# Token sums of the up-projection made ahead and kept in DRAM, in a hybrid block of 2,048 frames

## The chip, the cores and the metric

The kernel runs on one core of one Trainium2 chip. Its time is device microseconds for one launch, the median of several runs. Engines go by their names in the profile: PE (matrix products), DVE, ACT and POOL (elementwise work), SP (here the issuer of DMAs).

## The reference, cut to what matters

```
h  = h + concatenate([hgrn2(...), s5(...)]) @ w_out        # out tiles
hn = rmsnorm(h, ffn_norm_g)                                # (2048, 1024)
hid = hn @ w_up                                            # (1024 -> 2 x 2816)
hid = conv_b + sum(pad[:, j:j + seq_len] * conv_w[j] for j in range(3))
gate, val = split(hid, 2)
h  = h + (silu(gate) * val) @ w_down
```

All of it is float32.

## The kernel before, in words

The mixers run up to about 690 us, and then the projection with `w_out`. It goes in four blocks of 512 tokens, each of four out tiles (`out_tile`, 128 tokens, 48 matmuls). An out tile adds the residual, sums squares for the root mean square, and writes the tile to `h_d`. At the end of a block twelve operations on 128x4 (`rsqrt_mean`) make the scales `rst` of its tokens.

The up-projection runs in two halves of 1,024 tokens, 22 units each (`unit(hf, f)`). A unit makes 128 columns of the gate and 128 of the value. It does so with seven products, P1 to P7, of sums of weights and sums of tokens, in place of eight (Strassen's scheme in Winograd's form). With the tokens of a half in four parts B11, B12, B21 and B22 (first index: half of the model dimension; second: block of 512 tokens), the token factors are B11, B21, B22 and T1 = B12 − B11, T2 = B22 − T1, T3 = B22 − B12, T4 = B21 − T2. All factors stay in SBUF for a whole half, each as four tiles of 128x512 (index q). A matmul takes a float32 as a rounded part `h` and a rest `l`: `split` makes `h` by a copy on ACT and `l` by a subtraction on DVE or POOL. A product is twelve matmuls (four parts of the contraction by hh, lh and hl), so a unit has 84. `ps_u`, `ps_v` and `ps_w` are the PSUM banks of a unit: P1, P6, P7 and P4 go to u, P5 and P3 to v, P2 to w. P4 may start only when DVE has added P7 out of u (L62, `cv<-cv,ps_u`). `FACTOR` says which token factor a product takes: P1 B11, P2 B21, P5 T1, P6 T2, P3 B22, P7 T3, P4 T4.

The tokens come from `h_d`. For the first half, `h_load(0)` loads four tiles of 128x1024 during block 3's out tiles, ACT scales them, and `block_flips` turns them with PE (eight groups of four transposes, two in each out tile) and splits them as B11 and B21 (`nh`, `nl`). The other block of the half is turned in unit 0 by `token_sums`, four groups in P1 and four in P2, and for each q the sums are made: five on DVE and one on POOL, the splits of T1, T2 and T4 on DVE and those of B22 and T3 on POOL. For the second half the same is done in unit 21 (`block_flips`) and in the first unit of that half (`token_sums`). I call this place the change of tokens.

The sums of weights of the next unit are made during a unit by `unit_weights`: four sums (`us`) on POOL, five of the seven splits on DVE and two on POOL. The first unit's are made behind the last out tile (`first_up`).

A recording layer takes all operations, and a scheduler sets the order in which each engine gets them; from there every engine works in order. SP issues its DMAs in order too. `x_tile` has four buffers.

What PE needs of one q goes through load, scale, transposes, eviction, sum and split, in this order. The sum and split of T1 are:

```
sub(t1, b12, h11)
sub(t1, t1, l11)
part("T1", q, t1, VE)
```

## Time and profile before

| | us |
|---|---|
| median of 3 runs | 2310.33 (2306.52 to 2311.77) |
| the profiled execution | 2313.69 |
| its span in the trace | 2311.9 |
| PE busy | 2207.9 |
| DVE busy | 1712.9 |
| ACT busy | 990.7 |
| POOL busy | 765.6 |

The mean granted clock of PE is 0.977 of full speed. Where PE is busy without a break, the span is as long as its matmuls. Where it is not, the waits say which semaphore came last.

Stretches are told by the first matmul of a unit: block 3's out tiles begin at 845.95 us, unit 0 at 898.28, unit 4 at 1007.97, unit 21 at 1336.19, unit 26 (the fifth of the second half) at 1471.22, unit 43 at 1799.43.

### The profile page before, as it was taken

What the parts mean: (1) busy time and instruction counts of PE and PEld (TensorE: products, weight loads), DVE (VectorE), ACT (ScalarE), POOL (GpSimd) and SP (SyncE); (2) the same over time, 40 slices, a digit from 0 to 9 for tenths busy, and PEclk for the clock granted to TensorE, in tenths of its full rate; (3) what the DMA queues carried; (4) which work ended last, traced back from release to release, by engine and by line L of the source; (5) the groups of instructions that cost most, each with busy time, mean ns of one, the idle gap of its engine ahead of it and who ended that gap; (6) DMA issues with size and microseconds to landing.
All of it is one profiled execution on the core that took longest, in us unless ns stands there. A gap on an engine that the chain in (4) does not pass through costs nothing.

```text
span 2311.9 us, 28187 instructions
## 1 busy us (share of the span) xinstructions
PE 2207.9 (96%) x10120; PEld 1771.8 (77%) x10120; DVE 1712.9 (74%) x2615; ACT 990.7 (43%) x1770; POOL 765.6 (33%) x696
## 2 busy tenths in 40 slices
PE   8999999999989998899999988999999899999996
PEld 6778778888868876688888866888888677777775
DVE  9887786666664325887777778777777688788787
ACT  5333353232254334555555564555555423233343
POOL 1111100000000004555555555655555234445432
PEclk9899999999999999899999988999999999999998
DMA  6465655334434333222222222222222622222223
GB/s 226 143 210 178 188 183 162 124 125 131 141 87 136 116 119 109 83 97 83 83 80 82 78 91 82 93 82 82 83 82 73 227 83 84 71 90 75 68 88 119
DMA packets 143790, 262.18 MB, mean 113 GB/s; under 512 B 43936, under 2 KB 67360, under 8 KB 143648
## 3 DMA queue, kind: packets, MB, share of 16 engines
q1 hardware_dynamic: 138896, 243.05, 32.4%
q0 software_dynamic: 4752, 17.30, 2.0%
q8 instruction: 80, 1.31, 0.2%
q14 instruction: 62, 0.51, 0.1%
HBM read 178.52 MB, written 81.79 MB: 113 GB/s over the span
## 4 chain that ended last, share of the span: by engine, by line
PE 72%; DVE 16%; issue 5%; DMA 3%; ACT 2%; POOL 1%; SPq 0%; DVEq 0%; POOLq 0%; ACTq 0%
PE ps_u L1168 19%; PE ps_v L1168 9%; PE ps_out L975 6%; PE ps_du L1361 6%; PE ps_pj L231 5%; PE ps_pj L233 5%; PE ps_pj L232 5%; PE ps_w L1168 5%; PE ps_dv L1361 3%; DVE accp L62 2%; DVE gvl L65 2%; PE ps_dn L1448 1%; DMA graw<-gv_d 1%; DVE cv L65 1%; PE ps_att L649 1%
## 5 line engine op out<-in xcount | busy, mean ns | idle before, releaser
L231 PE MATMUL ps_pj<-xh,wh 128*128 128x512 f32 x640 | 261.9, 409 | 6.6 <-ACT xh L201 6.4
L232 PE MATMUL ps_pj<-xl,wh 128*128 128x512 f32 x640 | 256.4, 401 | 0.0
L233 PE MATMUL ps_pj<-xh,wl 128*128 128x512 f32 x640 | 256.0, 400 | 0.0
L74 DVE SCALAR_TENSOR_TENSOR cv<-cv,par 128x1024 f32<-128x1024 f32 x176 | 237.1, 1364 | 25.3 <-ACT cv L1180 23.4
L132 ACT ACTIVATE uh<-us 128x512 fp32r<-128x512 f32 x176 | 110.5, 630 | 195.6 <-PE ps_u L1168 93.4
L56 POOL TENSOR_TENSOR us<-uraw 128x512 f32<-128x512 f32 x88 | 121.8, 1384 | 215.4 <-DMA uraw<-in_wup_dram 149.7
L65 DVE TENSOR_TENSOR ul<-us,uh 128x512 fp32r<-128x512 f32 x132 | 156.2, 1184 | 1.6 <-ACT uh L132 1.5
L1361 PE MATMUL ps_du<-dh,gvh 128*128 128x512 f32 x320 | 131.9, 412 | 25.3 <-DVE accp L62 16.8
L132 ACT ACTIVATE uh<-uraw 128x512 fp32r<-128x512 f32 x132 | 83.5, 632 | 159.0 <-PE ps_u L1168 81.0
L231 PEld LDWEIGHTS ps_pj<-xh,wh 128*128 128x128 f32 x640 | 121.9, 190 | 37.2 <-ACT xh L201 6.4
L233 PEld LDWEIGHTS ps_pj<-xh,wl 128*128 128x128 f32 x640 | 121.6, 190 | 29.5 <-issue 1.1
L232 PEld LDWEIGHTS ps_pj<-xl,wh 128*128 128x128 f32 x640 | 121.7, 190 | 28.2 <-issue 1.5
L1361 PE MATMUL ps_du<-dl,gvh 128*128 128x512 f32 x320 | 128.6, 402 | 0.0
L1361 PE MATMUL ps_du<-dh,gvl 128*128 128x512 f32 x320 | 128.6, 402 | 0.0
L65 POOL TENSOR_TENSOR ul<-us,uh 128x512 fp32r<-128x512 f32 x44 | 68.6, 1560 | 173.0 <-ACT uh L132 170.6
L132 ACT ACTIVATE gvh<-gs 128x512 fp32r<-128x512 f32 x80 | 50.4, 630 | 162.3 <-POOL gs L56 81.6
L62 DVE TENSOR_TENSOR accp<-accp,ps_du 128x1024 f32<-128x1024 f32 (+1 forms) x84 | 97.7, 1163 | 28.7 <-PE ps_du L1361 28.3
L1180 ACT ACTIVATE cv<-cv,par 128x1024 f32<-128x1024 f32 x88 | 109.7, 1246 | 19.3 <-DVE cv L62 17.9
L56 POOL TENSOR_TENSOR gs<-graw 128x512 f32<-128x512 f32 x38 | 58.6, 1542 | 160.8 <-DMA graw<-gv_d 135.0
L1361 PEld LDWEIGHTS ps_du<-dh,gvh 128*128 128x128 f32 x320 | 61.7, 193 | 48.9 <-issue 23.8
L975 PE MATMUL ps_out<-wo,ogp 128*128 128x512 f32 x384 | 95.5, 404 | 0.9 <-DVE og L74 0.9
L515 POOL MEMSET z<- 128x4 f32 x16 | 1.7, 104 | 284.7 <-DVE zi L65 212.7
(438 smaller groups left out, 6237.4 us busy)
## 6 DMA issues: line engine op xcount, KB each, us to landing
uraw<-in_wup_dram SPq DMA_DIRECT2D x86, 512.0 KB, 3.5
gv_d<-cv SPq DMA_DIRECT2D x43, 512.0 KB, 2.6
graw<-gv_d SPq DMA_DIRECT2D x84, 256.0 KB, 3.3
wraw<-in_win_dram SPq DMA_DIRECT2D x24, 512.0 KB, 4.5
xt<-in_wdown_dram SPq DMA_DIRECT2D x44, 256.0 KB, 3.0
ws_d<-wh POOLq DMA_DIRECT2D x16, 512.0 KB, 3.5
ws_d<-wl POOLq DMA_DIRECT2D x16, 512.0 KB, 6.0
wh<-ws_d SPq DMA_DIRECT2D x16, 512.0 KB, 4.0
```

Source lines behind the costliest of these rows:

```text
L56: eng.tensor_tensor(o, a, b, op=op)
L62: eng.tensor_tensor(o, a, b, op=ALU.add)
L65: eng.tensor_tensor(o, a, b, op=ALU.subtract)
L74: eng.scalar_tensor_tensor(o, a, s, b, op0=op0, op1=op1)
L132: SC.activation(h, raw, AF.Copy)
L231: PE.matmul(ps, a, xh, start=(kt == 0), stop=False)
L232: PE.matmul(ps, a, xl, start=False, stop=False)
L233: PE.matmul(ps, b, xh, start=False, stop=(kt == KT - 1))
L975: PE.matmul(pss[nh], parts[lp][kt][:, tq], wo[rp][kt][:, nh * BLK : (nh + 1) * BLK], start=first, stop=last)
L1168: PE.matmul(ps, l, r[kt], start=(fresh and first), stop=end, skip_group_check=not fresh)
L1180: SC.activation(c, cin[:, 2 : HALF + 2], AF.Identity, scale=tap[2], bias=par[:, C_CB + cb : C_CB + cb + 1])
L1361: PE.matmul(ps[:, i], l[:, j, i * P : (i + 1) * P], r, start=(fresh and n == 0), stop=(n == 5), skip_group_check=not fresh)
```

## The change

New functions make the token sums apart from the place where they are used.

- `token_rows(hf, q)` does one q for both blocks of a half: it loads columns q and q+4 of the model dimension (128 each) for eight tiles of tokens (eight DMAs of 128x2x128, 128 KB, with ACT's scale of 256 columns behind each), turns them (four groups of four transposes, each with one ACT eviction), makes T1, T2, T4 and T3 with four subtractions on DVE, and writes T1, T2, B22, T3, T4 to `tr_d` in DRAM. For the first half B11 and B21 are split at once; for the second they are written too.
- `token_load` reads a tensor back, two tiles of 128x1024 each; `token_split` splits it, on ACT and DVE, in four parts.
- First half: the four q are made in the four out tiles of block 3. T1 and T2 are loaded back ahead of unit 0, and B22, T3 and T4 in unit 0. The sums and the two POOL splits of the first unit's weights go to DVE. The mean square of block 3 is recorded behind unit 0.
- Second half: q = 0 to 3 are loaded in units 2, 6, 10 and 14 and turned and summed in units 3, 7, 11 and 15. In unit 21 and the first unit of the second half there are only loads and splits: 28 of 128x512, all on DVE, with as many copies on ACT.

The diff:

```diff
--- before.py
+++ after.py
@@ -81,6 +81,8 @@
     h_d = dp.tile([SEQ, D], F32, name="h_d")
     gv_d = dp.tile([NF, P, SEQ], F32, name="gv_d")
     ws_d = [dp.tile([P, 2, KT * P], F32, name=f"ws_d{i}") for i in range(16)]
+    tr_d = [{k: dp.tile([P, 4, BLK], F32, name=f"tr_{k}{hf}") for k in ("B11", "B21", "T1", "T2", "B22", "T3", "T4")}
+            for hf in range(2)]
     m_d = dp.tile([8, 32 * 8 * (MS - 16) + MS], F32, name="m_d")
     tb_d = dp.tile([8, 4, P, 512], F32, name="tb_d")
 
@@ -114,19 +116,6 @@
 
     def halves(t):
         return [t[:, 0:BLK], t[:, BLK:D]]
-
-    def block_flips(xs, gcol, dst, pool, tag):
-
-        def one(kt):
...
     def split(raw, h, l, eng=GP):
         SC.activation(h, raw, AF.Copy)
@@ -985,16 +974,54 @@
             SC.activation(junk, xt[:, q], AF.Square, accum_out=ss[:, nh, i : i + 1])
         dma(h_d[t0 : t0 + P, :], xt)
 
-    def h_load(blk):
-
-        hs = []
-        for i in range(4):
-            t = 4 * blk + i
-            ht = x_tile()
-            dma(ht, h_d[t * P : (t + 1) * P, :])
-            SC.activation(ht, ht, AF.Copy, scale=rst[:, t : t + 1])
-            hs.append(halves(ht))
-        return hs
+    def token_rows(hf, q, pool, tag, first=None):
+
+        x, b = [], []
+
+        def load():
+            for j in range(2):
+                xt = x_tile().rearrange("p (i k c) -> p i k c", i=4, k=2)
+                for i in range(4):
+                    t = 8 * hf + 4 * j + i
+                    dma(xt[:, i], h_d[t * P : (t + 1) * P, :].rearrange("p (k q c) -> p k q c", k=2, q=4)[:, :, q])
+                    SC.activation(xt[:, i], xt[:, i], AF.Copy, scale=rst[:, t : t + 1])
+                x.append(xt)
+
+        def turned(j):
+            b.append(halves(x_tile()))
+            for k in range(2):
+                ps = pool.tile([P, BLK], F32, tag=tag, name="ps_x")
+                for i in range(4):
+                    PE.transpose(ps[:, i * P : (i + 1) * P], x[j][:, i, k], ident)
+                g = par[:, C_FFG + q + 4 * k : C_FFG + q + 4 * k + 1]
+                SC.activation(b[j][k], ps, AF.Copy, scale=g)
+
+        def sums():
+            (b11, b21), (b12, b22) = b
+            t1, t2 = halves(x_tile())
+            t3, t4 = halves(x_tile())
+            sub(t1, b12, b11)
+            sub(t2, b22, t1)
+            sub(t4, b21, t2)
+            sub(t3, b22, b12)
+            for k, t in dict(T1=t1, T2=t2, B22=b22, T3=t3, T4=t4).items():
+                dma(tr_d[hf][k][:, q], t)
+            for k, t in enumerate((b11, b21)):
+                if first:
+                    split(t, first[0][k][q], first[1][k][q], VE)
+                else:
+                    dma(tr_d[hf][("B11", "B21")[k]][:, q], t)
+
+        return [load, lambda: turned(0), lambda: turned(1), sums]
+
+    def token_load(hf, k):
+
+        rows = []
+        for p in range(2):
+            xt = x_tile()
+            dma(xt.rearrange("p (q t) -> p q t", q=2), tr_d[hf][k][:, 2 * p : 2 * p + 2])
+            rows += halves(xt)
+        return rows
 
     p3w = ExitStack()
     W3 = {}
@@ -1002,7 +1029,7 @@
 
     MAKE = ("P1", "P5", "P6", "P2", "P7", "P3", "P4")
 
-    def unit_weights(g, v):
+    def unit_weights(g, v, eng_s=GP):
 
 
 
@@ -1019,14 +1046,14 @@
 
         def summed(k, a, b, op, eng):
             s = tmp[k] = pool.tile([P, BLK], F32, tag="st", name="us", bufs=3)
-            tt(GP, s, a, b, op)
+            tt(eng_s, s, a, b, op)
             put(k, s, eng)
 
         ops = {
             "P1": lambda: put("P1", g[0], VE),
-            "P5": lambda: summed("P5", v[0], v[1], ALU.add, GP),
+            "P5": lambda: summed("P5", v[0], v[1], ALU.add, eng_s),
             "P6": lambda: summed("P6", tmp["P5"], g[0], ALU.subtract, VE),
-            "P2": lambda: put("P2", g[1], GP),
+            "P2": lambda: put("P2", g[1], eng_s),
             "P7": lambda: summed("P7", g[0], v[0], ALU.subtract, VE),
             "P3": lambda: summed("P3", g[1], tmp["P6"], ALU.subtract, VE),
             "P4": lambda: put("P4", v[1], VE),
@@ -1047,7 +1074,7 @@
         p2w.close()
         W3["pool"] = p3w.enter_context(tc.tile_pool(name="fw", reuse_waits="tile", bufs=2))
         r = W3["raw"]
-        W3["w"], ops = unit_weights(r[0:2], r[2:4])
+        W3["w"], ops = unit_weights(r[0:2], r[2:4], VE)
         for op in ops:
             op()
 
@@ -1055,7 +1082,7 @@
     parts[0] = og_parts(0)
     for cb in range(4):
         glu_out(y0, cb, pglu[cb], parts[0])
-    hn = [None, None]
+    hn = None
     for b in range(4):
         ss = sm.tile([P, 2, 4], F32, tag="hss", name="hss")
         weave = ()
@@ -1067,9 +1094,16 @@
                 raw = mx.tile([P, BLK], F32, tag=f"z{j % 2}{j // 2}", name="uraw")
                 dma(raw, A["wup"][j // 2].rearrange("p k c -> p (k c)")[:, (j % 2) * BLK : (j % 2 + 1) * BLK])
                 W3["raw"].append(raw)
-            hs = h_load(0)
-            hn[0] = first_tiles()
-            weave = block_flips(hs, C_FFG, hn[0], ps_s5, "s5")
+            hn = first_tiles()
+            rows = [token_rows(0, q, ps_s5, "s5", hn) for q in range(4)]
+            rows[0][0]()
+            weave = []
+            for q in range(4):
+                weave += [rows[q][1], rows[q][2]]
+                if q < 3:
+                    weave.append(lambda q=q: (rows[q][3](), rows[q + 1][0]()))
+                else:
+                    weave.append(rows[q][3])
         for i in range(4):
             out_tile(b, i, parts[b], ss, weave[4 * i : 4 * i + 4], first_up if (b, i) == (3, 3) else None)
             if b < 3:
@@ -1078,14 +1112,15 @@
                     gp = y_split(y)
                 for cb in ((), (0,), (1,), (2, 3))[i]:
                     glu_out(y, cb, glu_mm(gp, cb, ps_pj, "pj"), parts[b + 1])
-            elif i == 1:
-                hs = h_load(1)
         if b < 3:
             o = og_parts(b + 1)
             for p in range(2):
                 parts[b + 1][p] = o[p] + parts[b + 1][p]
         add(ss[:, 0], ss[:, 0], ss[:, 1])
-        rsqrt_mean(ss[:, 0], 4, D, "h", out=rst[:, 4 * b : 4 * b + 4])
+        rms = lambda b=b, ss=ss: rsqrt_mean(ss[:, 0], 4, D, "h", out=rst[:, 4 * b : 4 * b + 4])
+        if b < 3:
+            rms()
+    ahead = {k: token_load(0, k) for k in ("T1", "T2")}
     p2.close()
 
     if dbg == 2:
@@ -1107,53 +1142,13 @@
         def wide():
             return fx.tile([P, HALF + 2], F32, tag="cv", name="cv")
 
...
-        def token_sums(xs, first, tok):
-
-            tok.update({k: [[t[:, q] for q in range(4)] for t in
-                            (fb.tile([P, 4, BLK], F32R, tag=f"{k}{p}", name=f"t{k}{p}") for p in "hl")]
-                        for k in ("T1", "T2", "T3", "T4", "B22")})
...
+        def token_split(rows, k, dst):
+
+            if k not in dst:
+                t = [fb.tile([P, 4, BLK], F32R, tag=f"{k}{p}", name=f"t{k}{p}") for p in "hl"]
+                dst[k] = [[t[p][:, q] for q in range(4)] for p in range(2)]
+            for q in range(4):
+                split(rows[q], dst[k][0][q], dst[k][1][q], VE)
 
         FACTOR = {"P1": "B11", "P2": "B21", "P3": "B22", "P4": "T4", "P5": "T1", "P6": "T2", "P7": "T3"}
         NORMAL = ("P1", "P5", "P6", "P2", "P7", "P3", "P4")
@@ -1217,9 +1212,27 @@
             tok["B11"] = [first[p][0] for p in range(2)]
             tok["B21"] = [first[p][1] for p in range(2)]
 
+        def coming(hf, dst, order):
+
+            got = {}
+
+            def one(n):
+                if n:
+                    token_split(got.pop(order[n - 1]), order[n - 1], dst)
+                if n < len(order):
+                    got[order[n]] = token_load(hf, order[n])
+
+            return [(lambda n=n: one(n)) for n in range(len(order) + 1)]
+
+        for k in ("T1", "T2", "B22", "T3", "T4"):
+            for p in "hl":
+                fb.tile([P, 4, BLK], F32R, tag=f"{k}{p}", name=f"t{k}{p}")
         tok = {}
-        first_block(tok, hn[0])
-        sums = token_sums(hs, hn[0], tok)
+        first_block(tok, hn)
+        for k in ("T1", "T2"):
+            token_split(ahead[k], k, tok)
+        rest = coming(0, tok, ("B22", "T3", "T4"))
+        rows = [token_rows(1, q, ps_c, "x") for q in range(4)]
         w = W3["w"]
         for hf in range(2):
             for f in range(NF):
@@ -1230,20 +1243,26 @@
                 else:
                     w_next, ops = None, []
                 weave = {}
-                if f == 0:
-                    weave = {"P1": sums[0:4], "P2": sums[4:8]}
+                if f == 0 and hf == 0:
+                    weave = {k: [op] for k, op in zip(("P1", "P2", "P5", "P6"), rest)}
+                elif f == 0:
+                    weave = {"P1": [rest[5]], "P2": [rest[6]], "P5": [rest[7]]}
                 elif last and hf == 0:
-                    hs = h_load(2)
-                    nxt = first_tiles()
-                    fl = block_flips(hs, C_FFG, nxt, ps_c, "x")
-                    weave = {"P5": fl[0:2], "P6": fl[2:4], "P3": fl[4:6], "P7": fl[6:8]}
+                    nxt = {}
+                    first_block(nxt, first_tiles())
+                    rest = coming(1, nxt, ("B11", "B21", "T1", "T2", "B22", "T3", "T4"))
+                    rest[0]()
+                    weave = {k: [op] for k, op in zip(("P5", "P6", "P7", "P4"), rest[1:5])}
+                elif hf == 0 and f % 4 == 2 and f < 18:
+                    weave = {"P4": [rows[f // 4][0]]}
+                elif hf == 0 and f % 4 == 3 and f < 19:
+                    weave = {"P1": [rows[f // 4][1]], "P5": [rows[f // 4][2]], "P6": [rows[f // 4][3]]}
                 unit(hf, f, w, tok, EDGE if f == 0 or last else NORMAL, ops, weave)
                 w = w_next
+                if (hf, f) == (0, 0):
+                    rms()
                 if last and hf == 0:
-                    hs = h_load(3)
-                    tok = {}
-                    first_block(tok, nxt)
-                    sums = token_sums(hs, nxt, tok)
+                    tok = nxt
         pa.close()
```

Three places of the engines' order follow. The tiles `ul` are rests of weights, `us` the sums of weights, `tT1l` and the like rests of token factors, `cv` sums or convolution results, `x_...` a tile of the residual.

DVE behind the last out tile, before:

```order
L62 TENSOR_TENSOR x_8003<-x_8003,ps_out 128x512 x2
L65 TENSOR_TENSOR ul<-uraw,uh 128x512
L65 TENSOR_TENSOR ul<-us,uh 128x512 x3
L65 TENSOR_TENSOR ul<-uraw,uh 128x512
L62 TENSOR_TENSOR hss<-hss 128x4
L71 TENSOR_SCALAR rs_v<-hss 128x4
L69 TENSOR_SCALAR rs_i<-rs_v 128x4
L65 TENSOR_TENSOR ul<-uraw,uh 128x512
L71 TENSOR_SCALAR rst<-rs_i 128x4
L65 TENSOR_TENSOR cv<-cv,nh 128x512
L74 SCALAR_TENSOR_TENSOR rs_t<-rst 128x4
```

DVE ahead of and in unit 0, now:

```order
L65 TENSOR_TENSOR ul<-uraw,uh 128x512
L59 TENSOR_TENSOR rs_t<-rs_t,rs_v 128x4
L74 SCALAR_TENSOR_TENSOR rst<-rs_t,rst 128x4
L65 TENSOR_TENSOR tT1l<-xt,tT1h 128x512 x4
L65 TENSOR_TENSOR tT2l<-xt,tT2h 128x512 x4
L62 TENSOR_TENSOR cv<-cv,ps_w 128x512
L65 TENSOR_TENSOR ul<-us,uh 128x512
L65 TENSOR_TENSOR tB22l<-xt,tB22h 128x512 x4
L65 TENSOR_TENSOR tT3l<-xt,tT3h 128x512 x4
L62 TENSOR_TENSOR cv<-cv,ps_v 128x512
```

The sums and splits alternated with the mean square's operations; now the 128x4 operations stand ahead, and splits of T1, T2, B22 and T3 follow in fours, each four behind a load.

DVE at the change of tokens, in the last unit of the first half and the first of the second, before:

```order
L74 SCALAR_TENSOR_TENSOR cv<-cv,par 128x1024
L65 TENSOR_TENSOR cv<-cv,nh 128x512
L74 SCALAR_TENSOR_TENSOR cv<-cv,par 128x1024
L65 TENSOR_TENSOR cv<-cv,nl 128x512
L59 TENSOR_TENSOR cv<-cv 128x1024
L65 TENSOR_TENSOR tT1l<-cv,tT1h 128x512
L65 TENSOR_TENSOR cv<-cv 128x512
L65 TENSOR_TENSOR cv<-cv,nh 128x512
L65 TENSOR_TENSOR cv<-nh,cv 128x512
L65 TENSOR_TENSOR tT2l<-cv,tT2h 128x512
L62 TENSOR_TENSOR cv<-cv,nl 128x512
```

The same place now:

```order
L65 TENSOR_TENSOR tT2l<-xt,tT2h 128x512 x4
L65 TENSOR_TENSOR ul<-uraw,uh 128x512
L65 TENSOR_TENSOR tB22l<-xt,tB22h 128x512 x3
L74 SCALAR_TENSOR_TENSOR cv<-cv,par 128x1024
L65 TENSOR_TENSOR tB22l<-xt,tB22h 128x512
L74 SCALAR_TENSOR_TENSOR cv<-cv,par 128x1024
L65 TENSOR_TENSOR ul<-uraw,uh 128x512
L59 TENSOR_TENSOR cv<-cv 128x1024
L65 TENSOR_TENSOR tT3l<-xt,tT3h 128x512 x4
L62 TENSOR_TENSOR cv<-cv,ps_w 128x512
L65 TENSOR_TENSOR tT4l<-xt,tT4h 128x512 x4
L65 TENSOR_TENSOR ul<-us,uh 128x512
```

The subtractions on `cv` that make T1, T2 and T4 are gone; splits stand in fours, and the operations of the units (`ul`, L62, L74, L59) stand between them.

SP in the out tiles of block 3, before:

```order
L969 DMA x_7845<-in_x_dram 128x1024
L994 DMA xt<-h_d 128x1024
L986 DMA h_d<-x_7758 128x1024
L969 DMA x_7944<-in_x_dram 128x1024
L994 DMA xt<-h_d 128x1024
L986 DMA h_d<-x_7845 128x1024
L994 DMA xt<-h_d 128x1024 x3
L969 DMA x_8003<-in_x_dram 128x1024
```

The same place now (`tr_T_80`, `tr_T_81`, `tr_B_82`, `tr_T_83` and `tr_T_84` are the first half's T1, T2, B22, T3 and T4 in DRAM):

```order
L958 DMA x_7909<-in_x_dram 128x1024
L1008 DMA tr_B_82<-xt 128x512
L1008 DMA tr_T_80<-xt 128x512
L1008 DMA tr_T_81<-xt 128x512
L1008 DMA tr_T_83<-xt 128x512
L1008 DMA tr_T_84<-xt 128x512
L986 DMA xt<-h_d 128x2x128 x8
L975 DMA h_d<-x_7778 128x1024
L958 DMA x_8040<-in_x_dram 128x1024
L1008 DMA tr_T_80<-xt 128x512
```

For each q five writes of sums now stand ahead of the eight loads of the next q. On PE, P4 of unit 0 now stands behind 21 matmuls of unit 1, and P4 of the second half's first unit behind 8 matmuls of the next one.

## Rows read from the trace of the kernel before

**Rows 1.** Page, costliest groups and engines: busy us, mean ns, idle before, releaser.

```profile
PE 2207.9 (96%) x10120; PEld 1771.8 (77%) x10120; DVE 1712.9 (74%) x2615; ACT 990.7 (43%) x1770; POOL 765.6 (33%) x696
...
L74 DVE SCALAR_TENSOR_TENSOR cv<-cv,par 128x1024 f32<-128x1024 f32 x176 | 237.1, 1364 | 25.3 <-ACT cv L1180 23.4
```

**Rows 2.** Stretches: us, then each engine's busy us, PE's clock, DMA share, GB/s.

```profile
845.95:898.28 52.33, 50.14 (x225) 40.40 (x224) 13.46 (x20) 19.48 (x31) 6.34 (x5) 0.97 0.36 121
898.28:1007.97 109.69, 92.82 (x373) 70.93 (x372) 98.52 (x100) 61.16 (x96) 71.13 (x55) 0.91 0.24 82
1007.97:1336.19 328.22, 328.22 (x1430) 268.15 (x1429) 247.37 (x222) 166.86 (x239) 175.62 (x171) 1.00 0.25 82
1336.19:1471.22 135.03, 116.33 (x482) 88.59 (x480) 113.09 (x106) 74.54 (x111) 77.16 (x56) 0.90 0.26 90
1471.22:1799.43 328.21, 328.21 (x1429) 268.25 (x1428) 245.63 (x222) 166.81 (x238) 173.51 (x136) 1.00 0.23 79
```

**Rows 3.** PE's waits in units 0 to 3: us, times, longest.

```profile
PE ps_v L1168 <- DVE tT1l L65: 7.5, 4, 3.6
PE ps_u L1168 <- DVE tT2l L65: 3.7, 1, 3.7
```

**Rows 4.** PE's waits from unit 21 to unit 26.

```profile
PE ps_v L1168 <- DVE tT1l L65: 4.4, 2, 2.5
PE ps_u L1168 <- ACT cv L1192: 3.8, 2, 3.3
```

**Rows 5.** DVE by form from unit 21 to unit 26: busy us, mean ns.

```profile
L65 DVE TENSOR_TENSOR tT2l<-cv,tT2h 128x512 fp32r<-128x512 f32 x4 | 3.8, 951 | 0.0
...
L65 DVE TENSOR_TENSOR tT4l<-cv,tT4h 128x512 fp32r<-128x512 f32 x4 | 2.7, 680 | 0.0
```

**Rows 6.** Timeline of DVE and POOL in unit 0: start, us, operation.

```profile
909.63 0.68 DVE L65 TENSOR_TENSOR cv<-cv 128x512 f32<-128x512 f32 x1
909.65 1.79 POOL L56 TENSOR_TENSOR us<-us,uraw 128x512 f32<-128x512 f32 x1
...
910.24 1.22 DVE L74 SCALAR_TENSOR_TENSOR rst<-rs_t,rst 128x4 f32<-128x4 f32 x1
...
911.38 0.68 DVE L65 TENSOR_TENSOR cv<-cv,nh 128x512 f32<-128x512 f32 x1
...
911.40 1.78 POOL L56 TENSOR_TENSOR us<-uraw 128x512 f32<-128x512 f32 x1
```

**Rows 7.** Timeline of DVE and POOL at the change of tokens.

```profile
1374.44 1.75 DVE L65 TENSOR_TENSOR tT1l<-cv,tT1h 128x512 fp32r<-128x512 f32 x1
...
1375.60 1.73 POOL L65 TENSOR_TENSOR tT3l<-cv,tT3h 128x512 fp32r<-128x512 f32 x1
1376.11 1.76 DVE L65 TENSOR_TENSOR cv<-cv 128x512 f32<-128x512 f32 x1
```

**Rows 8.** Timeline of PE in the out tiles of block 3.

```profile
854.46 0.55 PE L123 MATMUL ps_x<-ident,xt 128*128 128x128 f32 x3 [2.19 <-ACT xt L995]
854.77 4.59 PE L975 MATMUL ps_out<-wo,zp 128*128 128x512 f32 x12
859.20 0.60 PE L123 MATMUL ps_x<-ident,xt 128*128 128x128 f32 x4
859.55 3.05 PE L975 MATMUL ps_out<-wo,zp 128*128 128x512 f32 x12
```

**Rows 9.** PE's waits in the out tiles of block 3.

```profile
PE ps_x L123 <- ACT xt L995: 2.2, 1, 2.2
```

**Rows 10.** DMAs on h_d: issue ns min/median/max, and landing us.

```profile
L994 SPq DMA_DIRECT2D xt<-h_d x16: 319/374/982, 831.0 to 1356.8; - x16
...
DMA to landing us min/median/max: 2.6/4.3/13.1
```

**Rows 11.** ACT from 845 to 1360: busy us, mean ns, idle before, releaser.

```profile
L995 ACT ACTIVATE xt<-xt,rst 128x1024 f32<-128x1024 f32 x10 | 11.5, 1146 | 8.2 <-DMA xt<-h_d 7.9
L126 ACT ACTIVATE nh<-ps_x,par 128x512 fp32r<-128x512 f32 x16 | 10.8, 686 | 18.5 <-PE ps_x L123 18.5
```

**Rows 12.** Timeline of DVE before block 3, with POOL idle.

```profile
843.31 0.17 DVE L71 TENSOR_SCALAR rst<-rs_i 128x4 int32<-128x4 int32 x1
```

More of the change, by code (lines that the diff above doesn't have):

```diff
@@ L116, in halves @@
         return [t[:, 0:BLK], t[:, BLK:D]]
-    def block_flips(xs, gcol, dst, pool, tag):
-        def one(kt):
-            ps = pool.tile([P, BLK], F32, tag=tag, name="ps_x")
-            for i in range(4):
-                PE.transpose(ps[:, i * P : (i + 1) * P], xs[i][kt // 4][:, (kt % 4) * P : (kt % 4 + 1) * P], ident)
-            g = par[:, gcol + kt : gcol + kt + 1]
-            h = dst[0][kt // 4][kt % 4]
-            SC.activation(h, ps, AF.Copy, scale=g)
-            stt(dst[1][kt // 4][kt % 4], ps, g, h.bitcast(F32), ALU.mult, ALU.subtract)
-        return [(lambda kt=kt: one(kt)) for kt in range(KT)]
     def split(raw, h, l, eng=GP):
@@ L986, in out_tile @@
         dma(h_d[t0 : t0 + P, :], xt)
-    def h_load(blk):
-        hs = []
-        for i in range(4):
-            t = 4 * blk + i
-            ht = x_tile()
-            dma(ht, h_d[t * P : (t + 1) * P, :])
-            SC.activation(ht, ht, AF.Copy, scale=rst[:, t : t + 1])
-            hs.append(halves(ht))
-        return hs
+    def token_rows(hf, q, pool, tag, first=None):
[39 more added lines that the diff above has]
+        return rows
     p3w = ExitStack()
```

36 lines of the change are left out of this document (removed).

## The prediction

> **What bounds the kernel now.** I read the page first: TensorE is busy 96% of the span [rows 1], so what can be won is mostly PE's idle time and slow clock, and the question is in which stretch they lie. The second view is the table by stretch [rows 2], cut at the first matmuls of units (unit 0 at 898.28, unit 4 at 1007.97, unit 21 at 1336.19, unit 26 at 1471.22): out tiles of block 3, units 0 to 3, units 4 to 20, unit 21 with the first four of the second half, and units 4 to 20 of that half. In the steady stretches PE is busy the whole time: 328.22 us for 17 units, 19.31 us a unit or 0.230 us a matmul at a granted clock of 1.00. Units 0 to 3 take 109.69 us, 32.5 over four times that pace, with the clock at 0.91; unit 21 and the next four take 135.03 us, 38.5 over five times the pace, at 0.90. These 71 us are all that the change can win here.
>
> The third view, PE's waits, says for what it waits there: splits of T1 and T2 on DVE head the list at the start [rows 3], T1's split and the end of ACT's copies at the change of tokens [rows 4]. The cause is DVE's load. A steady unit holds 247.37 / 17 = 14.55 us of DVE work, which leaves 4.76 us of 19.31. Units 0 to 3 hold 98.52 us, 40.3 more than four steady units; the change of tokens holds 113.09, again 40.3 more than five [rows 2]. In the 52.33 us of block 3's out tiles DVE works only 13.46 us. A price list of the splits and two close-ups of DVE beside POOL [rows 5 to 7] come last, since they decide how fast the work that stays can go.
>
> **The change, part by part.** The sum is made against the profiled execution, 2313.69 us; the median of the runs is 2310.33, so I subtract 3.4 at the end.
>
> (a) Out tiles of block 3. Each of the four now has 16 transposes in place of 8. Four cost 0.35 us of PE (from 859.20 to 859.55), so one costs 0.09 [rows 8], and 32 more cost 2.9 us. In before PE waits 2.2 us there for the scaled rows [rows 9], and the twelve matmuls after it take 4.59 us where others take 3.05 [rows 8]; I let both go, −3.7. What is late next: a chain per q, as the rows of q+1 are loaded only behind the writes of q. Eight issues of 0.374 us make 3.0, the landing 4.3 [rows 10], the last scale 0.3 (a quarter of 1.146 [rows 11]), transposes 0.35, three evictions at 0.69 [rows 11] 2.0, three subtractions at 0.68 (the cheapest 128x512 operation [rows 5]) 2.0, an issue 0.4: 12.4 us. A tile is 48 matmuls at 0.238, (52.33 − 2.9 − 3.7) / 192, and 16 transposes: 12.8 us. The cover is thin, and I put 2.2 for it, the wait of before; bounds 0, and four times 4 us if every landing is as late as 8.3. (a) is +1.4.
>
> (b) Units 0 to 3. The transposes and DVE's subtractions of the first half go; 20 splits of T1, T2, B22, T3, T4 stay, and DVE gains four sums and two splits of the first weights that were POOL's. Behind the last out tile DVE has 13 operations of 128x512 before T1's first split, and the twelve of 128x4 of the mean square. Where DVE and POOL alternate, a 128x4 takes 1.22 us [rows 6]; with POOL still it takes 0.17 [rows 12]. POOL has nothing to do there now, so I take 13 x 0.62 (the step from 909.63 to 910.24 [rows 6]) + 12 x 0.2 + 0.9 for ACT's copies = 11.4 us to T1's split. PE reaches T1 after some 7 us, and waits 4.4. From there to the addition of P7, for which P4 waits, DVE has 25 operations at 0.68 and two of 1.36 [rows 1]: 19.7, with 1.5 for the six POOL operations of the next weights, 32.6 us in all. P4 ends 2.8 later, at 35.4. By then PE has issued 105 matmuls (unit 0 and 21 of unit 1, ahead of P4 in its order), 24.1 us. So 11.3 us are lost, and 1.7 I add for the clock, since a PE that waits had 0.91 here: 13. Lower bound 6: 25.1 us of DVE work beyond steady units against 4 x 4.76 of room. Upper bound 20: the 27 operations at the 0.88 that half a POOL step makes [rows 6]. With the 16 transposes that unit 3 gains (1.4), (b) is 13 + 1.4 − 32.5 = −18.1.
>
> (c) Units 7, 11 and 15 gain 16 transposes each: 48 x 0.09 = +4.3. Their four subtractions (4 x 0.95 = 3.8) fit in the 4.76 us that DVE has; ACT's 8 scales and 4 evictions fit too, as ACT works 166.86 of 328.22 us [rows 2]. If they are not hidden, a row unit costs 5 us more. The loads of these rows stand on SP ahead of the unit's weights, eight issues or 3.0 us, covered by the two to three tiles of weights loaded ahead.
>
> (d) Change of tokens. The 64 transposes (5.8 us), 20 sums and eight of the two-part evictions on DVE go; 28 splits are left, all on DVE, the eight of B22 and T3 among them that were POOL's. At 0.95 [rows 5] they are 26.6 us in place of 40.3. From unit 21's start to the addition that P4 of the next unit waits for, DVE has 52 operations in order. At 0.90 to 1.17 each that is 47 to 61 us; PE needs 176 x 0.230 = 40.4 for what stands ahead of P4. The middle, 13.6, with 0.9 for the clock is 14.5 us lost. Lower bound 3 (26.6 against 5 x 4.76), upper 24 (61 − 40.4, and 3.3 for the clock). (d) is 14.5 − 38.5 = −24.0.
>
> The rest, up to the end of block 2 and the down projection, has the same order in both. Sum: 1.4 − 18.1 + 4.3 − 24.0 = −36.4, or 2277.3 against the profiled execution and 2274 on the median. No row before shows a 128 KB strided load of rows, nor a write and a read back within 10 us; for both I take the 4.3 of the whole rows [rows 10], the nearest, with 2.6 and 13.1 as ends.
>
> **A rule against it.** In the close-up at the start two DVE operations go to one of POOL [rows 6], at the change of tokens one to one, and a split takes 1.75 us [rows 7], though others of the same stretch take 0.95 and 0.68 [rows 5]. So POOL's sums slow a DVE that is packed with operations from SBUF, by an amount that depends on how the two fall into step.
>
> The Trainium skill has a rule on it (SBUF — State Buffer, Who interferes with whom): a DVE instruction with two SBUF inputs contends with a GpSimd instruction that reads SBUF, the shared pair of ports is an exclusive lock, and the one that comes second blocks fully. The close-up at the change of tokens agrees with it, the one at the start with two DVE operations to one of POOL only in part. By it the added splits would go one to one with POOL's sums.
>
> **The rivals.**
> 1. Lockstep. If each added split goes one to one with a POOL operation, 28 splits cost 1.75 − 0.95 = 0.80 more at the change of tokens, 22 us, and 20 at the start 16 us: 2274 + 38 = 2312, no change. For it: [rows 7]. Against: POOL works 71.13 of 109.69 us and 77.16 of 135.03 [rows 2], and the change takes its two or three splits per q away, so it can't stand beside every DVE operation. Chance 0.07.
> 2. The way through DRAM decides, and the kernel is slower. Eight landings lie in the chain one after another: four of the out tiles' loads, the last write and its reading back, and two of the later tensors' loads. Each us over 4.3 costs 8 us, so the win of 36.4 is gone from a landing of 8.9, and at 10 us the time is 2274 + 46 = 2320. For it: 13.1 is seen, these loads are pieces of 512 bytes, and SP issues in order, so that a write that waits for DVE holds up all loads behind it. Against: the median of 4.3 holds for tiles of four times the size [rows 10], and the DMA share in the stretch is 0.36 [rows 2]. Chance 0.11.
> 3. The row units aren't hidden: four units at 5 us in place of 1.4 make +14, 2288. Chance 0.14.
> 4. DVE packs well, both residues come out at their lower bounds: 2274 − 7 − 11.5 = 2255.5. Chance 0.14.
> That the change does not do what it says is no case: the order shows the sums gone from the start and from the change of tokens.
>
> **How the numbers follow.** The forecast, 2274 within about 12 us, has a chance of 0.54. The 8-in-10 range runs from rival 4's end to somewhat over rival 3, 2256 to 2304, and leaves out 0.18 above (rivals 1 and 2) and little below. A difference of 0.2% (4.6 us) is what can be told from no change; faster by more are the forecast and rivals 3 and 4, 0.82; within it rival 1, 0.07; slower rival 2, 0.11.
>
> **What would show it.** Unit 4's first matmul about 17 us before 1007.97, near 991; unit 21's 12 to 13 us before 1336.19 and unit 26's 37 before 1471.22 are the three steps, with the steady stretches still at 19.31 a unit. In PE's waits at the start T1's split comes first with 4 to 5 us, and P4 waits for the addition of P7; at the change of tokens P4 of the first unit of the second half waits for DVE, and that stretch has no transpose. Block 3 is to take 52 to 56 us; over 60 speaks for rival 2, as do waits of ACT for the loads of rows. A split that takes 1.7 us in most cases speaks for rival 1. The prediction is wrong if unit 4 starts after 1000 or the two residues together are over 45 us.

## The result, and the profile after

The changed kernel takes 2281.0 us (2278.41 to 2283.63), the kernel before 2310.2. The ratio is 0.9875, with a 95% interval of 0.9862 to 0.9888: 29 us faster, 7 us short of the forecast. The profiled execution takes 2280.0 us with a span of 2277.7, against 2313.69 and 2311.9.

The table by stretch comes first (block 3, units 0 to 3, 4 to 20, unit 21 to the fifth of the second half, and on to unit 43; columns as in [rows 2]).

```profile
846.41:899.68 53.27, 52.96 (x257) 41.86 (x256) 23.13 (x42) 31.71 (x64) 0.10 (x1) 1.00 0.67 216
899.68:996.33 96.65, 86.26 (x353) 66.70 (x352) 80.24 (x96) 58.94 (x101) 44.97 (x41) 0.95 0.52 172
996.33:1334.07 337.74, 334.51 (x1478) 272.85 (x1477) 261.69 (x235) 181.59 (x271) 188.89 (x172) 1.00 0.33 109
1334.07:1440.70 106.63, 99.93 (x422) 79.56 (x420) 95.04 (x94) 62.62 (x99) 64.40 (x45) 0.98 0.42 143
1440.70:1768.91 328.21, 328.21 (x1429) 268.20 (x1428) 245.37 (x222) 167.19 (x238) 170.16 (x134) 1.00 0.23 79
```

Against [rows 2] the four stretches that the change touches are +0.9, −13.0, +9.5 and −28.4 us, together −31.0. Up to block 3 the new execution is 0.5 later. From unit 26 to the end it takes 837.0 us against 840.7, although no order changes there. In the profiles of the twelve runs below that stretch takes 834.3 to 844.0, so those 3.7 us are no effect of the change. I compare by stretches for this reason.

The table shows more if idle time and slow clock are told apart. A matmul takes 0.230 us at full clock and a transpose 0.0985 (eight from 849.22 to 850.01). What PE's busy time has over that, I call slow; the rest of the stretch is idle time. The transposes are 32, 36, 0 and 60 in the four stretches before, and 64, 16, 48 and 0 after.

| us | idle before | slow before | idle after | slow after |
|---|---|---|---|---|
| block 3 | 2.2 | 2.8 | 0.3 | 2.5 |
| units 0 to 3 | 16.9 | 12.0 | 10.4 | 7.5 |
| units 4 to 20 | 0.0 | 0.1 | 3.2 | 1.6 |
| unit 21 to unit 25 | 18.7 | 13.9 | 6.7 | 3.4 |

In block 3 some 1.3 of what is called slow is there without a slow row as well: e2 below, with the order of before, has 48.59 us of busy time in it at a granted clock of 1.00. Outside block 3 each us of idle time came with 0.5 to 0.75 us of slower matmuls. The timeline of PE in unit 0 shows how.

```profile
906.58 0.39 PE L1163 MATMUL ps_w<-nl,uh 128*128 128x512 f32 x1
906.81 0.40 PE L1163 MATMUL ps_w<-nh,ul 128*128 128x512 f32 x1
910.51 0.79 PE L1163 MATMUL ps_v<-tT1h,uh 128*128 128x512 f32 x1 [3.30 <-ACT tT1h L121]
...
912.19 0.63 PE L1163 MATMUL ps_v<-tT1h,ul 128*128 128x512 f32 x1
912.61 0.63 PE L1163 MATMUL ps_v<-tT1h,uh 128*128 128x512 f32 x1
913.04 0.63 PE L1163 MATMUL ps_v<-tT1l,uh 128*128 128x512 f32 x1
```

PE waits from 907 to 910.51 for ACT's copy of T1, and then its matmuls come every 0.43 us, where they came every 0.23 before. The granted clock in that part, by the same view as the table by stretch, was 0.50, the lower of the two levels (1.2 GHz):

```profile
912.20:916.20 4.00, 4.00 (x11) 2.84 (x10) 4.00 (x3) 3.83 (x8) 3.92 (x3) 0.50 0.41 133
```

What PE waits for, the longest waits in the three stretches (units 0 to 2, units 4 to 20, unit 21 to 25):

```profile
PE ps_v L1163 <- ACT tT1h L121: 3.3, 1, 3.3
PE ps_u L1163 <- DVE cv L62: 2.7, 1, 2.7
```

```profile
PE ps_u L1163 <- ACT cv L1187: 3.2, 3, 1.5
```

```profile
PE ps_u L1163 <- DVE cv L62: 3.8, 1, 3.8
PE ps_u L1163 <- ACT cv L1187: 1.5, 2, 0.9
```

Of [rows 3] and [rows 4] the splits of T1 and T2 are gone from the head of the list. Five shorter waits for rests on DVE, 4.3 us together, are left in unit 0. P4 now waits for the addition of P7 in both places, and a wait for ACT stands in units 4 to 20, where there was none. DVE in unit 0:

```profile
910.85 4.67 DVE L65 TENSOR_TENSOR tT1l<-xt,tT1h 128x512 fp32r<-128x512 f32 x4
915.44 5.76 DVE L65 TENSOR_TENSOR tT2l<-xt,tT2h 128x512 fp32r<-128x512 f32 x4
...
922.83 2.49 DVE L65 TENSOR_TENSOR tB22l<-xt,tB22h 128x512 fp32r<-128x512 f32 x4
925.24 2.49 DVE L65 TENSOR_TENSOR tT3l<-xt,tT3h 128x512 fp32r<-128x512 f32 x4
...
935.83 0.67 DVE L62 TENSOR_TENSOR cv<-cv,ps_u 128x512 f32<-128x512 f32 x1
```

T1's first split starts 11.2 us after unit 0 begins (forecast 11.4). The eight splits of T1 and T2 take 1.17 and 1.44 us each, those of B22 and T3 0.62: beside the first eight POOL makes the sums of unit 1's weights. The addition starts at 36.2 and ends at 36.8 (forecast 32.6, with the addition). At the change of tokens, in unit 21:

```profile
1347.23 2.48 DVE L65 TENSOR_TENSOR nl<-xt,nh 128x512 fp32r<-128x512 f32 x4
...
1350.24 1.28 DVE L65 TENSOR_TENSOR tT1l<-xt,tT1h 128x512 fp32r<-128x512 f32 x2
...
1352.04 1.29 DVE L65 TENSOR_TENSOR tT1l<-xt,tT1h 128x512 fp32r<-128x512 f32 x2
...
1353.84 2.29 DVE L74 SCALAR_TENSOR_TENSOR cv<-cv,par 128x1024 f32<-128x1024 f32 x1
1356.06 0.68 DVE L62 TENSOR_TENSOR cv<-cv,ps_u 128x512 f32<-128x512 f32 x1
```

P7's last matmul is issued at 1350.4, but its addition stands behind two splits of T1, one of weights and a step of the convolution, and starts at 1356.06: 3.8 us of waiting for P4, of unit 21 and not of the unit behind it.

ACT in units 7 and 8:

```profile
1073.68 0.51 ACT L987 ACTIVATE xt<-xt,rst 128x256 f32<-128x256 f32 x1 [1.88 <-DMA xt<-h_d]
1074.81 1.78 ACT L987 ACTIVATE xt<-xt,rst 128x256 f32<-128x256 f32 x4 [0.61 <-DMA xt<-h_d]
...
1077.02 0.90 ACT L987 ACTIVATE xt<-xt,rst 128x256 f32<-128x256 f32 x2
...
1078.97 0.49 ACT L987 ACTIVATE xt<-xt,rst 128x256 f32<-128x256 f32 x1
...
1083.17 0.58 ACT L1187 ACTIVATE cv<-ps_u 128x512 f32<-128x512 f32 x1
```

These are the scales of the next q (L987), eight in 6 us and partly behind their loads, and the copy of unit 8's P1 that they delay (L1187). The loads are recorded in unit 10, and SP issues them at 1069.11, in unit 7: the scheduler has moved them ahead, which I put down to free x buffers.

### The profile page after: what moved, and what is told of

Read it like the earlier page. It is cut to its first block, busy times and chain, and to the rows that moved or that the text cites. A ratio compares the mean times of both kernels' runs of the same rounds, so it can differ in the third digit from the quotient of the medians.

```text
span 2277.7 us, 28419 instructions
## 1 busy us (share of the span) xinstructions
PE 2194.5 (96%) x10120; PEld 1764.9 (77%) x10120; DVE 1700.9 (75%) x2629; ACT 1006.0 (44%) x1834; POOL 730.3 (32%) x666
## 3 DMA queue, kind: packets, MB, share of 16 engines
q1 hardware_dynamic: 164368, 268.23, 36.3%
## 4 chain that ended last, share of the span: by engine, by line
PE 70%; DVE 17%; DMA 5%; issue 4%; ACT 3%; SPq 1%; POOL 1%; DVEq 0%; POOLq 0%; ACTq 0%
PE ps_u L1163 18%; PE ps_v L1163 9%; PE ps_out L964 7%; PE ps_pj L220 5%; PE ps_pj L222 5%; PE ps_du L1380 5%; PE ps_pj L221 5%; PE ps_w L1163 5%; PE ps_dv L1380 2%; DVE accp L62 2%; DMA graw<-gv_d 2%; PE ps_dn L1467 2%; DVE gvl L65 2%; PE ps_att L638 1%; DVE cv L74 1%
## 5 line engine op out<-in xcount | busy, mean ns | idle before, releaser
L74 DVE SCALAR_TENSOR_TENSOR cv<-cv,par 128x1024 f32<-128x1024 f32 x176 | 237.7, 1368 | 19.8 <-ACT cv L1175 17.9
L62 DVE TENSOR_TENSOR accp<-accp,ps_du 128x1024 f32<-128x1024 f32 (+1 forms) x84 | 97.7, 1164 | 28.7 <-PE ps_du L1380 28.6
L964 PE MATMUL ps_out<-wo,ogp 128*128 128x512 f32 x384 | 100.1, 409 | 0.9 <-DVE og L74 0.9
L964 PE MATMUL ps_out<-wo,zp 128*128 128x512 f32 x384 | 92.7, 397 | 0.0
```

Source lines behind the costliest of these rows:

```text
L62: eng.tensor_tensor(o, a, b, op=ALU.add)
L74: eng.scalar_tensor_tensor(o, a, s, b, op0=op0, op1=op1)
L964: PE.matmul(pss[nh], parts[lp][kt][:, tq], wo[rp][kt][:, nh * BLK : (nh + 1) * BLK], start=first, stop=last)
```

## The experiments

The edits are cut to the lines that matter. Stretches in us (block 3; units 0 to 3; 4 to 20; unit 21 to 25), from the same view of each run:

```
before     52.33  109.69  328.22  135.03
after      53.27   96.65  337.74  106.63
e1         52.97   93.46  328.22  133.76
e2         50.13  110.42  338.61  105.61
e3         53.82   96.68  337.14  106.54
e4         53.24   93.06  337.64  106.46
e5         53.12  100.86  340.44  106.63
e6         53.41   94.49  337.99  106.90
e7         54.55   95.92  337.33  106.66
e8         53.59   94.17  344.95  106.11
e9         64.27   94.59  337.45  106.92
e10        52.96   90.16  339.47   97.55
e11        53.36   96.99  337.85  106.45
e12        52.85   95.01  337.96  106.75
```

How well a stretch repeats: the change of tokens takes 106.45 to 106.92 us in the eight kernels beside after that leave it alone. Units 0 to 3 repeat less well: e8 has after's order there up to unit 3 and takes 2.5 us less; its splits of T1 take 2.50 us together in place of 4.67 and those of T2 6.86 in place of 5.76, as they meet POOL's sums. So in that stretch less than 2.5 us is no difference. Where e1 and e2 keep the order of before, its stretches come out at 133.76 (135.03), 110.42 (109.69) and, for block 3, 50.13 (52.33), so the 0.9 of block 3 is within what executions differ by.

**One half each.** e1 has `token_rows` and `token_load` for the first half alone, e2 for the second alone; the other half is as in the kernel before.

> Only the first half's part of the change: the change of tokens is as in the kernel before, and no rows are made in units 3, 7, 11 and 15. My theory: the parts add, since each stretch pays for its own DVE work. Units 0 to 3 then take 95 us or a little less (no transposes in unit 3), units 4 to 20 take 328.2, the change of tokens 135.0: about 13 us under the kernel before, some 2297. Rival: the parts are tied (by the shared x buffers and SP's queue), and the first alone wins under 8 or over 18 us.

> Only the second half's part: the start is as in the kernel before, the rows of the second half are made in units 3, 7, 11 and 15 and loaded at the change of tokens. My theory: units 4 to 20 cost 9.5 us more than in the kernel before, unit 3 some 1.7, and the change of tokens 28.4 less: 17 us under the kernel before, some 2293. Rival: with the start's backlog on DVE, unit 3's rows are late and the rows cost more, a gain under 12 us.

e1 has a ratio of 0.9945 (0.9930 to 0.9960), which is −12.7 us. Units 0 to 3 win 16.2, 3.2 more than in after, 1.8 of which are unit 3's transposes there. The change of tokens stays at 133.8. e2 wins 29.4 at the change of tokens and loses 10.4 in units 4 to 20, as after does. So the parts add stretch by stretch. By time e2 wins only 0.9965 (0.9953 to 0.9976), 8 us, where its stretches sum to −20.5; its profile has 844.0 us behind unit 26, 3.3 over before's. The rest lies in the executions that are compared: the profiled one of before, at 2313.69, is 8.7 over the median 2305.0 of before's runs timed beside e2, and the profiled one of e2 1.6 under e2's median.

**First weights back on POOL.**

```diff
-        W3["w"], ops = unit_weights(r[0:2], r[2:4], VE)
+        W3["w"], ops = unit_weights(r[0:2], r[2:4])
```

> The kernel after with the four sums and two splits of the first unit's weights back on POOL. My theory: POOL's six operations of 1.4 to 1.8 us run one behind the other and slow DVE's 128x4 operations again to 1.2 us, so that T1's first split comes 4 to 8 us later than now (910.85) and the kernel is 4 to 8 us slower, about 2287. Rival: T1's copies on ACT wait for the load of the third weight tile until 909.8 anyway, and DVE has six operations fewer (3.7 us): no change within 2 us.

0.9887 (0.9869 to 0.9906), units 0 to 3 at 96.68: the rival holds. T1's split comes 8.4 us after unit 0 begins, 2.8 earlier than in after, but PE waits 2.9 us for a rest of weights in the first product and 3.7 for B22's split, ahead of which four operations of the mean square take 1.14 to 1.25 us each beside POOL's sums. The addition of P7 ends 32.9 us after unit 0 begins, 3.9 earlier than in after, and the stretch is no shorter: DVE's queue up to that addition is not the only thing that holds PE there. This part of the change was worth nothing that can be told from the spread.

**POOL's sums in unit 0 left out.**

```diff
+            if plain:
+                tmp[k] = a
+                put(k, a, eng)
+                return
             s = tmp[k] = pool.tile([P, BLK], F32, tag="st", name="us", bufs=3)
```

> The kernel after without the four weight sums that POOL makes in unit 0 for unit 1 (unit 1 takes single weights in place of the sums). My theory: they stand beside the eight splits of T1 and T2, which take 1.17 and 1.44 us each where DVE alone takes 0.60; without them these go at 0.60 to 0.65, P4 of unit 0 starts 5 us earlier, and the kernel is 4 to 5 us faster, about 2276. Rival: the loads of B22, T3 and T4 set P4's start; then DVE only waits longer for them and the gain is 1 us or less.

The timeline of DVE in e4, the splits of T1 and T2:

```profile
908.77 2.49 DVE L65 TENSOR_TENSOR tT1l<-xt,tT1h 128x512 fp32r<-128x512 f32 x4
911.19 2.49 DVE L65 TENSOR_TENSOR tT2l<-xt,tT2h 128x512 fp32r<-128x512 f32 x4
```

0.9869 (0.9855 to 0.9884); the eight splits go at 0.62, half of after's time and less, 5.5 us less in all, the addition of P7 ends 32.2 us after unit 0 begins, and units 0 to 3 are 3.6 us shorter than in after. That is my theory for the splits; for the stretch the price is less sure, since e8, with the sums in place, is only 1.1 us longer than e4. The Trainium skill's rule (SBUF — State Buffer, Who interferes with whom) that a DVE instruction with two SBUF inputs contends with a POOL instruction that reads SBUF agrees with the splits of after and e4.

**Loads and scales.** e5 puts the row scales of the second half on POOL, e11 four of eight:

```diff
-                    SC.activation(xt[:, i], xt[:, i], AF.Copy, scale=rst[:, t : t + 1])
+                    if hf:   # e11: if hf and j:
+                        ts(xt[:, i], xt[:, i], rst[:, t : t + 1], ALU.mult, eng=GP)
+                    else:
+                        SC.activation(xt[:, i], xt[:, i], AF.Copy, scale=rst[:, t : t + 1])
```

> The kernel after with the eight scales of each row load of the second half on POOL in place of ACT. My theory: the waits of PE for ACT's copy of P1 in units 4, 8, 12 and 16 (1.3, 1.8, 1.1 and 0.1 us over the pace) come from eight scales of 0.45 us in ACT's queue ahead of that copy; with the scales on POOL they go, units 4 to 20 take 334 in place of 337.7 us, and the kernel is 3 to 4 us faster, about 2277. Rival: the scales then hold up the sums of weights on POOL, or slow DVE, and PE waits for weights instead: no gain.

> The kernel after with four of the eight scales of each row load of the second half on POOL and four on ACT. My theory: eight in one engine's queue are too many at once, on ACT (4.3 us lost in units 4, 8, 12, 16) as on POOL (7 us lost in units 4 to 20); with four on each both have room and units 4 to 20 take 334 to 335 us in place of 337.7. Rival: the scales on POOL slow DVE and the sums of weights whatever their number: 337 or more.

e5: 0.9904 (0.9889 to 0.9919), units 0 to 3 are 4.2 and units 4 to 20 2.7 us longer; e11: 0.9882 (0.9867 to 0.9897), 337.85. Both rivals hold. On POOL such a scale takes 1.4 us where ACT takes 0.5, beside DVE. PE's waits for the copy of P1 in e5, in units 5, 9, 10 and 13:

```profile
1022.98 0.50 PE L1166 MATMUL ps_u<-tT2h,uh 128*128 128x512 f32 x1 [0.81 <-ACT cv L1190]
...
1104.21 0.50 PE L1166 MATMUL ps_u<-tT2h,uh 128*128 128x512 f32 x1 [0.81 <-ACT cv L1190]
...
1124.68 0.50 PE L1166 MATMUL ps_u<-tT2h,uh 128*128 128x512 f32 x1 [0.85 <-ACT cv L1190]
...
1185.93 0.50 PE L1166 MATMUL ps_u<-tT2h,uh 128*128 128x512 f32 x1 [0.82 <-ACT cv L1190]
```

With the scales off ACT the waits of units 4, 8 and 12 are gone, which supports ACT's burst as their cause. In their place stand these, for the same copy; ahead of that of unit 9 ACT itself waits 1.9 us for a step of the convolution on DVE. No run took the burst away without adding work elsewhere.

e6 leaves six read-backs out:

```diff
-                    got[order[n]] = token_load(hf, order[n])
+                    got[order[n]] = token_load(hf, order[n]) if hf else ahead[order[n]]
```

> The kernel after without the six loads of B22, T3 and T4 of the first half in unit 0: their splits take the tiles of T1 and T2, which are there already. My theory: DVE is the bound from T1's split to the addition of P7, and waits only 1.1 us for ACT's copies of T4, so the gain is 1 to 2 us. Rival: reading back sets the pace (ACT waits 7.2 us for these tiles): the kernel is 5 us or more faster.

0.9883 (0.9866 to 0.9901); units 0 to 3 are 2.2 us shorter, no more than the stretch's own spread. The rival's 5 us are not there: reading these three back in unit 0 is no bound.

**The margin of the chain through DRAM.** e7 doubles each load of rows in block 3.

```diff
+                    if not hf:
+                        dma(dup_d[8 * q + 4 * j + i], src)
```

> The kernel after with each of the 32 loads of rows in block 3's out tiles made twice (the second copy goes to DRAM, nothing waits for it). An issue takes 0.65 us there, so each q's chain is 5.2 us longer. My theory, that the cover was thin (12.4 against 12.8 us): a tile takes 4 to 5 us longer in each of the three where the next q is loaded, 12 to 15 us in all, about 2294. Rival: the chain has room, since PE waited 0.3 us only: within 3 us.

0.9869 (0.9854 to 0.9885), but it tested nothing: the scheduler moved the copies into blocks 1 and 2 (first 695.8, last 794.3 us). So e9 puts ten writes of sums in each chain, which can't move.

```diff
+            if first and q < 3:
+                for n in range(10):
+                    dma(dup_d[10 * q + n], b22[:, 0:256])
```

> The kernel after with ten more writes of 128x256 to DRAM (nothing reads them) on SP behind the five writes of each q, ahead of the eight loads of the next q in block 3's out tiles: some 4 us more of issues in the chain of each of three q. The doubled loads of the run before did not test this, since they were put into the blocks before. My theory now: the chain has some room, since PE waited 0.3 us there, but not 4 us: block 3 takes 58 to 65 us in place of 53.3. Rival: the room is over 4 us, block 3 stays within 2 us of 53.3, and the forecast's thin cover was wrong.

Block 3 in the table by stretch of e9, and then PE's longest wait in it:

```profile
845.61:909.88 64.27, 55.43 (x257) 43.03 (x256) 27.05 (x48) 34.60 (x70) 0.10 (x1) 0.94 0.71 234
```

```profile
PE ps_x L996 <- ACT xt L988: 7.5, 3, 7.0
```

0.9906 (0.9889 to 0.9922). The ten writes take SP 4.98, 6.38 and 4.91 us, 16.3 in all, and block 3 is 11.0 longer, so 5.3 us were absorbed. That is no room in each tile: of the three waits one is 7.0, ahead of the last q, as the order puts the transposes of the other two later. In after 24 matmuls, 5.7 us, stand behind the last transposes of the block, and here none. The transposes of q = 2 and q = 3 begin at 885.26 and 904.43, 19.2 apart, which without the 4.9 of writes between them leaves about 14.3 for the chain, where in after they begin 13.3 apart. By this estimate a chain takes as long as a tile: the cover is as thin as the forecast had it, or thinner.

**Splits made ahead.** e8 splits B11 and B21 of the second half in the row units.

```diff
+                    hl = halves(x_tile(F32R))
+                    split(t, *hl, VE)
+                    for p in range(2):
+                        dma(bs_d[p][k][:, q], hl[p].bitcast(F32))
```

> The kernel after with B11 and B21 of the second half split in the row units, kept in DRAM as h and l, and loaded ready at the change of tokens: eight splits fewer on DVE and eight copies fewer on ACT there, two and two more per row unit. My theory: DVE's queue in unit 21 makes P4 wait 3.8 us for the addition of P7; eight operations of 0.93 us fewer take that wait away, and the change of tokens gets 4 to 6 us shorter, while each row unit costs up to 1 us more: about 2278. Rival: loads decide there (ACT waits 6.9 us for tiles), and 2 MB in place of 1 for B11 and B21 delay T1's loads: no gain or slower.

The first matmul of P4 in e8, in unit 21 and in the unit behind it, and PE's longest wait in units 4 to 20:

```profile
1353.68 0.49 PE L1167 MATMUL ps_u<-tT4h,uh 128*128 128x512 f32 x1
...
1378.71 0.80 PE L1167 MATMUL ps_u<-tT4h,uh 128*128 128x512 f32 x1 [5.28 <-DVE cv L62]
```

```profile
PE ps_u L1167 <- ACT cv L1191: 7.8, 4, 2.6
```

0.9911 (0.9891 to 0.9931). The change of tokens is 0.5 us shorter and units 4 to 20 7.2 longer, with 7.8 us of waiting for ACT's copy of P1. The eight splits are gone, and so is the wait of unit 21, as my theory has it. But P4 of the next unit now waits 5.3 us for its own addition of P7, which ends 43.9 us after unit 21 begins, in after 45.6: the wait has moved one unit on, to where the forecast had put it, and DVE's whole queue up to that addition is what counts.

**No rests, no mean square.** e10 leaves the subtractions of the token splits out, e12 the mean square of block 3.

```diff
-                split(rows[q], dst[k][0][q], dst[k][1][q], VE)
+                SC.activation(dst[k][0][q], rows[q], AF.Copy)
```

> The kernel after without the subtractions of the token splits in unit 0 and at the change of tokens (20 and 28 on DVE; the rounded part is used in place of the rest). Loads, copies on ACT and all else stay. My theory: DVE's queue is the bound in both stretches. Then unit 0 to unit 4 takes 84 to 88 us in place of 96.65, and the change of tokens 97 to 100 in place of 106.6. Rival: the loads through four x buffers and ACT's copies are the bound: 94 and 104 or more.

Units 0 to 3 and the change of tokens in the table by stretch of e10:

```profile
896.38:986.54 90.16, 82.51 (x353) 65.33 (x352) 65.94 (x76) 58.45 (x101) 46.16 (x41) 0.98 0.55 184
1326.01:1423.56 97.55, 96.96 (x421) 78.71 (x420) 73.90 (x66) 62.64 (x99) 57.97 (x41) 1.00 0.45 157
```

0.9811 (0.9795 to 0.9827). The change of tokens takes 97.55, 1.0 over the pace: nearly all that is left there hangs on DVE's 28 splits (x buffers come free earlier without them too, which this run does not tell apart from DVE's time). Units 0 to 3 take 90.16, between the two theories: the 20 splits there hold 6.5 us of the 19.4 over the pace. PE still waits 3.3 us for T1's copy on ACT.

```diff
-                    rms()
+                    ts(rst[:, 12:16], rst[:, 8:12], 1.0, ALU.mult)
```

> The kernel after without the mean square of block 3 (its scales are those of block 2): twelve operations of 128x4 fewer on DVE ahead of T1's splits. My theory by the forecast's sum (0.2 us each in DVE's queue): T1's first split and the addition of P7 come 2.4 us earlier and units 0 to 3 take 94 to 95 us. Rival: P5 waits for ACT's copies of T1, which stand behind the copy of a weight tile loaded late (909.3), so DVE only has 2.4 us of idle time and units 0 to 3 stay at 96 to 97.

0.9866 (0.9850 to 0.9882), 95.01: 1.6 us shorter, within the spread, though also the upper end of my theory. T1's split starts 11.1 us after unit 0 begins and the addition of P7 at 36.3, as in after (11.2 and 36.2): DVE is early and waits 2.4 us for ACT's copy of a weight tile, as the rival has it.

No run is clearly faster than after with the same computation.

## Why the prediction was right, and where it was off

The mechanism was the forecast's: DVE's work at the start and at the change of tokens made PE wait, taking it away gave back most of that, as e1, e2 and e10 show, and 2281.0 lies 7 us over the 2274. Of the signs that it named, unit 4 began at 996.33, later than the 991 and short of the limit of 1000, unit 21 only 2.1 us before 1336.19 in place of 12 to 13, and unit 26 30.5 before 1471.22 in place of 37. By its steps:

- (a) Block 3, forecast +1.4, measured +0.9. The 32 transposes cost 3.2, against 2.9. The wait of before went, but of the slow matmuls only 0.3, so 2.5 us in place of 3.7, and a new wait of 0.3 came in place of 2.2. Two prices of the chain were off. The loads of rows in block 3, and below them the loads of whole rows in before, by their lines alone:

```profile
L986 SPq DMA_DIRECT2D xt<-h_d x24: 531/610/671, 857.6 to 889.3; - x24
...
DMA to landing us min/median/max: 2.6/3.0/3.5
```

```profile
L994 SPq DMA_DIRECT2D xt<-h_d x16: 319/374/982, 831.0 to 1356.8; - x16
...
DMA to landing us min/median/max: 3.4/5.2/7.0
```

An issue of these strided loads takes 0.61 us, not 0.374 [rows 10], and they land in 3.0. The 4.3 that I took for whole rows is the median of all DMAs on `h_d`, writes included; the loads alone took 5.2. Rival 2 is so answered: neither these landings nor those of the tensors read back (at most 7.7) come to 8.9.
- (b) Units 0 to 3, forecast −18.1, measured −13.0. The way to T1's first split was right (11.2 us, forecast 11.4). The term that failed is DVE's time from there to the end of the addition of P7, for which P4 waits: 21.2 forecast, 25.7 measured. The eight splits of T1 and T2 took 10.3 of it beside POOL's sums, where 0.68 each makes 5.4. The 1.7 for the clock was about right in the place where the sum has it: P4 itself took 4.4 us in place of 2.8. The other slow matmuls of the 7.5 stand ahead of P4, whose start waits for DVE, and lie within DVE's time. The 11.3 of the forecast counts all that is lost up to the end of P4, not idle time alone; measured are 17.2. The order of waits was not quite right either: P5 waits for T1's copy on ACT and not for the split on DVE. And the upper bound of 20 does not come out of its working: 27 operations at 0.88 make some 17, clock and POOL's 1.5 included, and 17.8 us were lost in the stretch.
- (c) Units 4 to 20, forecast +4.3, measured +9.5. The transposes are 1.75 us a row unit, 5.2. The other 4.3 are units 4, 8, 12 and 16 at 1.3, 1.8, 1.1 and 0.1 over the pace. The failed sentence is "ACT's 8 scales and 4 evictions fit too, as ACT works 166.86 of 328.22 us": an average said nothing on a burst that the order puts ahead of a copy PE needs, as the timeline of units 7 and 8 and e5 show it.
- (d) Change of tokens, forecast −24.0, measured −28.4. The splits went at 0.68 to 1.35 us. The term that failed is the price of DVE's 52 operations up to the addition of P7 in the first unit of the second half: 0.90 to 1.17 each, for which no row stands, so 54 us in the middle. They took 45.6, 0.88 each:

```profile
1378.98 0.68 DVE L62 TENSOR_TENSOR cv<-cv,ps_u 128x512 f32<-128x512 f32 x1
```

```profile
1379.71 0.50 PE L1163 MATMUL ps_u<-tT4h,uh 128*128 128x512 f32 x1
```

The wait that I named, P4 of that unit, is not there, as PE had lost its time before, at P4 of unit 21, and came just when the addition ended; e8 shows it where unit 21 does not wait. The sum has a slip too: the 176 matmuls, 40.4 us, hold P4's own twelve, and 164 (37.7 us) stand ahead of it, so that 54 us mean 16.3 lost and not 13.6. By luck the slip made the error smaller.
- Rival 1 (lockstep) is seen in part for the eight splits at the start, at a price of 1.1 to 3.6 us (e4 against e8 and after), not 16; in e8 and e12 the four of T2 go at 1.7 each. At the change of tokens those of T4 went at 1.35, the others mostly at 0.68 to 0.95. Rival 3 came true in part, by ACT and not by DVE, with 4.3 us over the transposes in place of 14.

So the errors were −0.5, +5.1, +5.2 and −4.4 us, together 5.4 of the 7 us that the forecast missed: errors of both signs left a small sum, and that it is so small is luck.

## What to carry to other kernels

Price a wait of PE with the slow matmuls behind it: here each us of waiting came with 0.5 to 0.75 us more. Slow matmuls that stand ahead of a further wait are no extra cost, as they only shorten that wait (P4 of unit 0). Before work is put into a stretch with room, look in the order of each engine at what stands behind the burst, since the average share of busy time does not show it. An operation taken from a packed engine can only move the wait: in e8 it went from one unit to the next, as the engine's queue up to the later addition was hardly shorter.
